# A hybrid recurrent, retention and convolution block on one core: activation operands made in parts, values in single banks, a weight unit queued behind the last norm

## The chip, the cores and the metric

The kernel runs on one core of one Trainium2 chip. The metric is the device time of one execution in microseconds (us); lower is better. A core has TensorE (PE: matmuls, with weight loads shown apart as PEld), VectorE (DVE), ScalarE (ACT), GpSimd (POOL) and SyncE (SP, which issues the DMAs here). Each works through its own queue in order. Matmuls write to PSUM, which has eight banks of 512 float32 columns on each of 128 partitions; everything else lies in SBUF.

## The reference

One layer over 528 tokens (16 meta tokens and 512 of the sequence), width 1024. All inputs are float32.

```python
xn = rms_norm(h, norm_mix_g[l])
z = xn @ w_in[l]
u_rnn, u_gate, q, k, v, g_ret, ga, gb = jnp.split(z, IN_SPLITS, axis=-1)
xr = causal_dwconv(u_rnn, rnn_conv_w[l], rnn_conv_b[l])
hr = rg_lru(xr, ...)
o_a = hr * jax.nn.gelu(u_gate)
q = rotary(q, pos); k = rotary(k, pos) * (RET_DK ** -0.5)
o = retention(q, k, v)
o_b = head_rms(o) * jax.nn.silu(g_ret)
mixed = sigmoid(ga) * (o_a @ w_branch_rnn[l]) + sigmoid(gb) * (o_b @ w_branch_ret[l])
h = h + mixed @ w_out[l]
xn = rms_norm(h, norm_ffn_g[l])
up = causal_dwconv(xn @ w_up[l], ffn_conv_w[l], ffn_conv_b[l])
gate, val = jnp.split(up, 2, axis=-1)
h = h + (jax.nn.gelu(gate) * val) @ w_down[l]
out = rms_norm(h, norm_final_g)[:, N_META:]
```

There are four retention heads with 512 values each; the feed-forward width is 3072, so `w_up` has 6144 columns (gates, then values).

## The kernel before

Every matmul runs on float16. An operand is split into a high and a low half, `hi` on ACT (line 92) and the rest `lo` on DVE (line 93), in the helper `split`; a product is the sum of three float16 products. Weights come in units of up to 1 MB, loaded by SP into two raw buffers (`wraw`), each load issued behind the one before it, and split into tiles `wt` of a pool of ten (`wsp`). `get(u)` makes all splits up to unit u at that point of the program, `tick()` makes one more step if not too many tiles are ahead.

Some products are Strassen forms: seven products of sums of blocks in place of eight. Their weight units are marked `fast`, have four tiles and need three sums on DVE (lines 255 to 257).

The program is traced in Python order. Up to line 713 the order on PE, ACT and DVE is the traced one; from there on a scheduler fixes each engine's order ahead of time, by the program's order (its priority), by what it takes to be ready, and by explicit edges. `tc.high_priority()` moves instructions ahead, `tc.issue_after(x)` queues those of the block that are on x's engine behind x, without a wait for x's result. A tile pool of PSUM, SBUF or raw buffers makes the next user of a slot wait for the last one.

The places that the change and the prediction touch, in order of time:

- `values(h)`, from line 884 on, the values of one head: five blocks of up to 128 tokens by 512 columns. Blocks 0 to 3 take 24 matmuls each (line 907), block 4, the last 16 tokens, 16 small ones (line 899) that read every weight tile of the head. Two blocks share a two-bank tile of the pool `acc`: block 0 and 1, 2 and 3. Each block is then split to `v` (lines 92 and 93). From head 2 on, PSUM is laid out as two such tiles and four single banks of the pool `bank`; the gates' products (`pa`, `pe`, `pb` of `fast_products`, line 844) take the single banks. Heads run as `gated(0)`, `values(2)`, `gated(1)`, `values(3)`, `gated(2)`.
- `out_proj(i)`, lines 1172 to 1189, for four blocks of 128 tokens: product (line 1180), residual `h` (line 1185), and the second norm's rows by `norm_rows`: Square and Sqrt on ACT (lines 343, 345), reciprocal and the two halves of `xo` on DVE (lines 347, 353). PE transposes `xo` later in `out_norm` (line 360). The loop after it calls `tick()` once for each block.
- Then `early`: three half products (line 408) with the first up unit `u_up[0][0]` (two) and the second, `u_up[0][1]` (one). The last norm's transposes are queued behind the second half product.
- The up projection, a loop over j = 0 to 11. Units j = 3, 5, 7, 9 (`FAST_UP`) form the gates by `up_products`: seven products (line 1319) into `pa`, `pe`, `pb`. `pa` is built up further after each copy of its state by ACT (`keep`, line 1325, into `kept`, `last`, `g`), and DVE adds (`add`, line 1329). The values use plain products (line 395). Convolutions are at lines 1295 and 1297, gelu at line 1311, gate times value at 1384 or 1395.
- At the end of each j, `act_forms` makes the operands of the down projection: four differences `d`, `y` of 256 columns on DVE (lines 1261 to 1264), and splits of A11 (256 columns) and of A12/A22, `y` and `d` (512 columns each) into `a` and `act`. They are used only by the down projection, after j = 11.

Of the kernel before, what the change touches and what calls it, by code (L numbers as in the profile page):

```python
# [9 lines left out]
F16 = mybir.dt.float16  # L10
AF = mybir.ActivationFunctionType
# [3 lines left out]
P = 128  # L15
# [36 lines left out]
def hybrid_block_kernel(ctx, tc, x, meta, norm_mix_g, w_in, conv_w, conv_b, rg_a_w, rg_a_b,  # L52
# [21 lines left out]
    def acc(name):  # L74
        return psum["acc"].tile([P, 2, 512], F32, name=name, tag="acc")
# [219 lines left out]
    def tick(n=1):  # L295

        for _ in range(n):
            if done[0] == len(steps):
                if len(loaded) == len(units):
                    return  # L300
                queue(unit_load())
            u = steps[done[0]][0]
            if sum(unit_tiles(i) for i in range(current[0], u + 1)) > ahead[0]:
                return
            emit_step()
# [34 lines left out]
    def rms_scale(src, rows, name):  # L340
        junk = work.tile([P, D], F16, name="junk", tag="w")
        ss = small.tile([P, 1], F32, name="ss")
        nc.scalar.activation(junk[:rows], src, AF.Square, accum_out=ss[:rows])
        sd = small.tile([P, 1], F32, name="sd")
        nc.scalar.activation(sd[:rows], ss[:rows], AF.Sqrt, scale=1.0 / D, bias=eps_t[:rows])
        rs = small.tile([P, 1], F32, name="rs")
        nc.vector.reciprocal(rs[:rows], sd[:rows])
        return rs

    def norm_rows(src, rows, g_bc, xn):  # L350
        rs = rms_scale(src, rows, "n")
        for a in range(2):
            nc.vector.scalar_tensor_tensor(xn[a][:rows], src[:, a * 512:(a + 1) * 512], rs[:rows], g_bc[a][:rows],
                                           op0=ALU.mult, op1=ALU.mult)

    def norm_transpose(rows, xhd, xld, s, xn):
        for a in range(2):
# [526 lines left out]
    def values(h):  # L884
        vt = []
        wa, wb = get(u_v[h][0]), get(u_v[h][1])
        for b, (j0, nb) in enumerate(JB):
            if b % 2 == 0:
                ps = acc("ps")
            pb = ps[:, b % 2]  # L890
            vt.append(piece([P, 2, 512], F16, f"v{h}"))
            i = 0
            if b == 4:
                for r, wr in enumerate((wa, wb)):
                    for a in range(2):
                        for g in range(4):
                            m = 2 * NM if a == 0 else NM
                            xs = xlast[:, 4 * r + g].rearrange("p a t -> p (a t)")
                            nc.tensor.matmul(pb[32 * g:32 * g + m], xs[:, :m], wr(a, g, 0, 512),
                                             start=r == 0 and a == 0, stop=r == 1 and a == 1,  # L900
                                             tile_position=(0, 32 * g))
                split(vt[b][:, 0], vt[b][:, 1], pb, S_V / (SW * S_XN))
                continue
            for k in range(KD):
                w = wa if k < 4 else wb
                for ax, aw in SPLIT:
                    nc.tensor.matmul(pb, xf(ax, k, XF + j0, nb), w(aw, k % 4, 0, 512), start=i == 0, stop=i == 23)  # L907
                    i += 1
            split(vt[b][:, 0], vt[b][:, 1], pb, S_V / (SW * S_XN))
            tick()  # L910
        vv[h] = vt
# [257 lines left out]

    psum_layout(bank=2, acc=3)  # L1170

    def out_proj(i):
        ps = acc("ps")
        halo = acc("ps") if i == 1 else None
        c0 = 2 + P * i
        ks = (0, 1, 2, 3, 4, 5, 7, 6) if i == 0 else range(KD)
        for k in ks:
            for n in range(2):
                for a, aw in SPLIT:
                    nc.tensor.matmul(ps[:, n], mx[k][:, a, c0:c0 + P], wo[k // 2](aw, k % 2, n * 512, 512),  # L1180
                                     start=k == 0 and (a, aw) == (0, 0), stop=k == ks[-1] and a == 1)
                if halo is not None:
                    halo_part(halo, k, 4 * n)
        hv = h2[i].rearrange("p (a b) -> p a b", a=2)
        nc.vector.scalar_tensor_tensor(hv, ps, 1.0 / (SW * S_MX), hv, op0=ALU.mult, op1=ALU.add)
        xn = pair("xo")
        with tc.high_priority():
            norm_rows(h2[i], P, gffn, xn)
        return xn, halo

    def out_norm(i, xn):
# [36 lines left out]
    for i in range(1, 4):  # L1228
        xn, halo = out_proj(i)
        xns.append(xn)  # L1230
        if i == 1:
            halo_sum(halo)
        out_norm(i - 1, xns[i - 1])
        tick()
        if i == 2:
            halo_finish()
    x2_whole(0)
# [6 lines left out]

    early = {}
    for ch, (u, col) in enumerate(((u_up[0][0], 0), (u_up[0][0], P), (u_up[0][1], 0))):
        wv = get(u)
        early[ch if ch < 2 else KF] = ps = acc("ps")
        mm = project_half(ps, wv, col, x2f, HU, 0)
        if ch == 1:  # L1250
            with tc.high_priority(), tc.issue_after(mm):
                out_norm(3, xns[3])
# [3 lines left out]
    def act_forms(j, vals):  # L1256


        (h1, h2_), (t0, t1) = halves, vals
        d, y = gates_t("d"), gates_t("y")  # L1260
        nc.vector.tensor_tensor(d[:, h2_], t0[:, h2_], t1[:, h2_], op=ALU.subtract)
        nc.vector.tensor_tensor(y[:, h1], t0[:, h1], t0[:, h2_], op=ALU.subtract)
        nc.vector.tensor_tensor(d[:, h1], t0[:, h1], d[:, h2_], op=ALU.subtract)
        nc.vector.tensor_tensor(y[:, h2_], d[:, h1], t1[:, h1], op=ALU.subtract)
        if j % 2 == 0:
            a11_t.append(piece([P, 2, SEQ], F16, "a11"))
        a11 = a11_t[-1][:, :, 256 * (j % 2):256 * (j % 2) + 256]
        split(a11[:, 0], a11[:, 1], t0[:, h1], S_ACT)
        at = {"A11": (a11, 0)}
        if j >= 10:  # L1270
            if j == 10:
                a21_t.append(piece([P, 2, SEQ], F16, "a21"))
            a21 = a21_t[0][:, :, 256 * (j % 2):256 * (j % 2) + 256]
            split(a21[:, 0], a21[:, 1], t0[:, h2_], S_ACT)
            at["A21"] = (a21, 0)
        for src, s, nms in ((t1, S_ACT, ("A12", "A22")), (y, S_ACT, ("F7", "F3")), (d, -S_ACT, ("F6", "F5"))):
            t = piece([P, 2, SEQ], F16, "act")
            split(t[:, 0], t[:, 1], src[:, :SEQ], s)
            at.update({nm: (t, 256 * i) for i, nm in enumerate(nms)})
        acts.append(at)  # L1280

    def gates_t(name):
        return work.tile([P, T], F32, name=name, tag="w")
# [30 lines left out]
    def up_products(w):  # L1314

        def product(ps, wf, xf_, first=False):
            for k in range(4):
                for aw, ax in SPLIT:
                    nc.tensor.matmul(ps[:, :258], w(wf, aw, k), x2_form(xf_, ax, k),  # L1319
                                     start=first and k == 0 and (aw, ax) == (0, 0), stop=k == 3 and aw == 1,  # L1320
                                     skip_group_check=True)

        def keep(dst, ps):
            with tc.high_priority():
                nc.scalar.activation(dst, ps[:, :258], AF.Copy)

        def add(dst, ps, k):
            with tc.high_priority():
                nc.vector.tensor_tensor(dst, ps[:, :258], k, op=ALU.add)

        kept, g0, g1 = (piece([P, 2, 258], F32, nm) for nm in ("kept", "g0", "g1"))
        last = piece([P, 258], F32, "last")
        pa = acc("pa")[:, 0]
        product(pa, "B11", "A11", True)
        keep(kept[:, 0], pa)
        yield
        pe = bank("pe")
        product(pe, "T3", "F7", True)
        yield
        product(pa, "T2", "F6")  # L1340
        keep(kept[:, 1], pa)
        yield
        pb = bank("pb")
        product(pb, "B21", "A12", True)
        add(g0[:, 0], pb, kept[:, 0])
        yield
        product(pa, "T1", "F5")
        keep(last, pa)
        add(g1[:, 1], pe, last)
        yield  # L1350
        product(pa, "B22", "F3")
        keep(g1[:, 0], pa)
        yield g1
        product(pe, "T4", "A22")
        add(g0[:, 1], pe, kept[:, 1])
        yield g0

    forming = []

    def forms(n):  # L1360
        for _ in range(n if forming else 0):
# [2 lines left out]
    for j in range(12):  # L1364
# [6 lines left out]
        gates, vals = [], []  # L1371
        if j in FAST_UP:
            run = up_products(wg)
            for _ in range(5):
                next(run)
                tick()
            vals.append(up_conv(wu, 0, KF + 2 * j))
            tick()
# [6 lines left out]
        else:  # L1385
# [4 lines left out]
            for m in range(2):  # L1390
# [5 lines left out]
                vals.append(cv)  # L1396
                tick()
                forms(1)
        act_forms(j, vals)


    ahead[0] = 9
# [178 lines left out]
```

## Time and profile before

| | |
|---|---|
| median of 3 runs | 1072.78 us (1072.77 to 1072.82) |
| profiled execution | 1072.88 us, span 1071.2 us |
| PE busy | 1051.1 us (98%) |
| PEld busy | 851.3 us (79%) |
| DVE busy | 863.1 us (81%) |
| ACT busy | 584.1 us (55%) |
| granted TensorE clock, mean | 0.999 |

The span runs from the first to the last instruction of the program; the rest of the profiled execution's time lies around it. Busy times are of each engine's own instructions; an idle engine that nobody waits for costs nothing.

### The profile page before, as it was taken

The page shows a single profiled execution, that of the slowest core. Times are in us where ns is not written, and L with a number is a line of the kernel's source. Part 1 is how long each engine was busy: PE and PEld are TensorE (multiplying, and loading weights), DVE is VectorE, ACT ScalarE, POOL GpSimd, SP SyncE. Part 2 cuts the span into 40 slices and gives each one's busy share as a digit, 9 for nine tenths or more (in the row PEclk, how much of TensorE's full clock was granted, in tenths as well). Part 3 has the DMA queues.
Part 4 walks back from the last instruction along what each step waited for, and adds up shares of the span by engine and source line. Part 5 has one row for each costly group of instructions (what it writes and reads, how often), then busy time and mean ns, then how long its engine had stood idle before and what let it go on. Part 6 is the DMA issues. An engine that isn't in the chain of part 4 may idle for free.

```text
span 1071.2 us, 20996 instructions
## 1 busy us (share of the span) xinstructions
PE 1051.1 (98%) x8995; PEld 851.3 (79%) x8995; DVE 863.1 (81%) x1297; ACT 584.1 (55%) x903; POOL 6.9 (1%) x20
## 2 busy tenths in 40 slices
PE   9999999999999999999999999999999999999997
PEld 6888888865684858888888885588888888888884
DVE  6884799998786969877797785599888887988875
ACT  8558954434564747566454453364555465454442
POOL 2000000000000000000000000000000000000000
PEclk9999999999999999999999999999999999999999
DMA  8341243431212222423333355032331423214322
GB/s 254 105 133 41 80 138 119 159 120 40 80 41 69 90 64 65 128 90 119 103 104 119 119 199 176 33 124 74 126 119 62 137 80 119 80 59 131 107 80 79
DMA packets 108990, 111.49 MB, mean 104 GB/s; under 512 B 5611, under 2 KB 100561, under 8 KB 108897
## 3 DMA queue, kind: packets, MB, share of 16 engines
q1 hardware_dynamic: 108448, 109.74, 31.8%
q8 instruction: 70, 1.15, 0.5%
q10 hardware_dynamic: 160, 0.27, 0.1%
q0 software_dynamic: 288, 0.14, 0.1%
q14 instruction: 24, 0.19, 0.1%
HBM read 108.04 MB, written 2.10 MB: 103 GB/s over the span
## 4 chain that ended last, share of the span: by engine, by line
PE 73%; DVE 16%; ACT 9%; issue 2%; ACTq 0%; DVEq 0%
PE ps L395 28%; PE P L1417 9%; PE pa L844 9%; PE pm L395 4%; PE ps L907 4%; PE ps L1180 4%; DVE wt L93 4%; PE pe L844 4%; PE ps L408 2%; PE pb L844 2%; ACT wt L92 2%; PE pa L1319 2%; PE ps L929 1%; DVE rnn L642 1%; DVE raw L255 1%
## 5 line engine op out<-in xcount | busy, mean ns | idle before, releaser
L395 PEld LDWEIGHTS <-wt 128*128 128x128 f16 x3840 | 373.2, 97 | 58.2 <-DVE t L736 1.4
L93 DVE SCALAR_TENSOR_TENSOR wt<-raw,wt 128x1024 f16<-128x1024 f32 (+2 forms) x278 | 303.8, 1105 | 69.1 <-ACT wt L92 68.0
L92 ACT ACTIVATE wt<-raw 128x1024 f16<-128x1024 f32 (+2 forms) x278 | 262.9, 961 | 152.6 <-PE P L1417 25.3
L844 PEld LDWEIGHTS <-wt 128*128 128x128 f16 x2016 | 195.1, 97 | 34.7 <-issue 7.4
L395 PE MATMUL ps<-x2h,wt 128*128 128x258 f16 x1184 | 182.0, 273 | 0.0
L395 PE MATMUL ps<-xh,wt 128*128 128x257 f16 (+2 forms) x1056 | 163.8, 275 | 1.1 <-DVE t L736 1.1
L395 PE MATMUL ps<-x2l,wt 128*128 128x258 f16 x592 | 113.3, 272 | 0.0
L395 PE MATMUL ps<-xl,wt 128*128 128x257 f16 (+2 forms) x528 | 102.2, 275 | 0.0
L1417 PE MATMUL P<-wt,act 128*128 128x256 f16 x792 | 88.3, 273 | 0.0
L1417 PEld LDWEIGHTS <-act 128*128 128x128 f16 x792 | 77.5, 98 | 9.0
L907 PE MATMUL ps<-wt,xh 128*128 128x512 f16 x256 | 76.1, 379 | 2.3 <-DVE v L93 2.3
L844 PE MATMUL pa<-xs,wt 128*128 128x257 f16 x576 | 71.6, 273 | 3.4 <-ACT kept L849 3.1
L1297 DVE SCALAR_TENSOR_TENSOR cv<-ps,vt,cv 128x512 f32<-128x512 f32 x80 | 59.7, 746 | 16.5 <-ACT cv L1295 15.8
L395 PE MATMUL pm<-oa,wt 128*128 128x257 f16 x480 | 55.4, 274 | 0.0
L907 PEld LDWEIGHTS <-xh 128*128 128x128 f16 x256 | 24.8, 98 | 31.4 <-issue 3.4
L907 PE MATMUL ps<-wt,xl 128*128 128x512 f16 x128 | 48.3, 379 | 0.0
L255 DVE TENSOR_TENSOR raw<-raw 128x1024 f32<-128x1024 f32 x39 | 47.6, 1220 | 0.7
L844 PE MATMUL pa<-ob,wt 128*128 128x257 f16 x384 | 45.7, 274 | 0.6 <-ACT last L849 0.5
L1180 PE MATMUL ps<-wt,mx 128*128 128x512 f16 x192 | 44.3, 379 | 0.0
L1295 ACT ACTIVATE cv<-ps,vt,vt 128x512 f32<-128x512 f32 x40 | 30.8, 769 | 23.4 <-PE ps L395 18.5
L1319 PEld LDWEIGHTS <-wt 128*128 128x128 f16 x336 | 32.6, 97 | 8.5 <-issue 4.1
L1180 PEld LDWEIGHTS <-mx 128*128 128x128 f16 x192 | 17.6, 98 | 18.5
(288 smaller groups left out, 1414.6 us busy)
## 6 DMA issues: line engine op xcount, KB each, us to landing
raw<-in_w_in SPq DMA_DIRECT2D x40, 1024.0 KB, 4.9
raw<-in_w_up SPq DMA_DIRECT2D x24, 1024.0 KB, 5.3
raw<-in_w_down SPq DMA_DIRECT2D x48, 256.0 KB, 3.5
raw<-in_w_branch_ret SPq DMA_DIRECT2D x16, 512.0 KB, 4.6
raw<-in_w_branch_rnn SPq DMA_DIRECT2D x8, 640.0 KB, 4.7
raw<-in_w_out SPq DMA_DIRECT2D x4, 1024.0 KB, 5.1
xin<-in_x SPq DMA_DIRECT2D x4, 512.0 KB, 5.8
raw<-in_w_in SPq DMA_DIRECT2D x4, 512.0 KB, 8.3
```

The lines of the kernel that those rows point to most:

```text
L92: nc.scalar.activation(hi, src, AF.Copy, scale=s)
L93: nc.vector.scalar_tensor_tensor(lo, src, s, hi, op0=ALU.mult, op1=ALU.subtract)
L255: nc.vector.tensor_tensor(pair, pair, rv[:, :, right].rearrange("p (h k) c -> p h k c", h=2), op=ALU.add)
L395: nc.tensor.matmul(ps[:, hf, :n], w(aw, k, col, P), src(ax, k, c0, n), start=k == 0 and (aw, ax) == (0, 0), stop=k == nk - 1 and aw == 1)
L408: mm = nc.tensor.matmul(ps[:, hf, :n], w(aw, k, col, P), src(ax, k, c0, n), start=k == 0 and (aw, ax) == (0, 0), stop=k == KD - 1 and aw == 1)
L844: nc.tensor.matmul(ps[:, :257], ws[k // 4](wf, aw, k % 4), src(xf_, ax, k), start=first and k == 0 and (aw, ax) == (0, 0), stop=k == last_ ...
L907: nc.tensor.matmul(pb, xf(ax, k, XF + j0, nb), w(aw, k % 4, 0, 512), start=i == 0, stop=i == 23)
L1180: nc.tensor.matmul(ps[:, n], mx[k][:, a, c0:c0 + P], wo[k // 2](aw, k % 2, n * 512, 512), start=k == 0 and (a, aw) == (0, 0), stop=k == ks ...
L1295: nc.scalar.activation(vv_, src[:, :, 2:258], AF.Identity, scale=vt2[:, 96 + ch:97 + ch], bias=bias)
L1297: nc.vector.scalar_tensor_tensor(vv_, src[:, :, j:j + 256], vt2[:, 48 * j + ch:48 * j + ch + 1], vv_, op0=ALU.mult, op1=ALU.add)
L1319: nc.tensor.matmul(ps[:, :258], w(wf, aw, k), x2_form(xf_, ax, k), start=first and k == 0 and (aw, ax) == (0, 0), stop=k == 3 and aw == 1, ...
L1417: nc.tensor.matmul(pd[:, 256 * tt:256 * tt + 256], t[:, ax, c0 + tt * P:c0 + tt * P + P], w(wf, aw, i), start=q % 6 == 0 and tt == 0 and i ...
```

## The change

In `act_forms` the work is put into three functions: `differences` (the four differences), `plain` (A11, A21 where there is one, and A12/A22) and `formed` (`y` and `d`). They go on a list. If the next j is not in `FAST_UP` they run at once, in the order in which they stood; if it is, `flush` runs the first behind the fourth of the next j's products and the other two behind the fifth, queued behind the latest copy on ACT and the latest sum on DVE. For heads 2 and 3 `values` takes one single bank for each block in place of half a two-bank tile. `norm_rows` returns its Sqrt and its last DVE instruction; the loop's `tick()` is left out for the last block, and the splits of `u_up[0][1]` are queued behind those two instructions.

```diff
-        nc.scalar.activation(sd[:rows], ss[:rows], AF.Sqrt, scale=1.0 / D, bias=eps_t[:rows])
+        root[0] = nc.scalar.activation(sd[:rows], ss[:rows], AF.Sqrt, scale=1.0 / D, bias=eps_t[:rows]).ins
...
+        return root[0], rr.ins
...
-            if b % 2 == 0:
-                ps = acc("ps")
-            pb = ps[:, b % 2]
+            if h >= 2:
+                pb = bank("pv")
+            else:
+                if b % 2 == 0:
+                    ps = acc("ps")
+                pb = ps[:, b % 2]
...
-            norm_rows(h2[i], P, gffn, xn)
+            behind[0] = norm_rows(h2[i], P, gffn, xn)
...
-        tick()
+        if i < 3:
+            tick()
...
-        wv = get(u)
+        if ch < 2:
+            wv = get(u)
+        else:
+            with tc.issue_after(behind[0][0]), tc.issue_after(behind[0][1]):
+                wv = get(u)
...
+        return [differences, plain, formed]
...
-                nc.scalar.activation(dst, ps[:, :258], AF.Copy)
+                last_copy[0] = nc.scalar.activation(dst, ps[:, :258], AF.Copy).ins
...
-                nc.vector.tensor_tensor(dst, ps[:, :258], k, op=ALU.add)
+                last_sum[0] = nc.vector.tensor_tensor(dst, ps[:, :258], k, op=ALU.add).ins
...
+    def flush(n):
+
+        for _ in range(min(n, len(pending))):
+            with tc.issue_after(last_copy[0]), tc.issue_after(last_sum[0]):
+                pending.pop(0)()
...
-            for _ in range(5):
+            for n in range(5):
                 next(run)
+                if n in (3, 4):
+                    flush(n - 2)
                 tick()
...
-        act_forms(j, vals)
+        pending.extend(act_forms(j, vals))
+        if j + 1 not in FAST_UP:
+            while pending:
+                pending.pop(0)()
```

## Rows read from the trace of the kernel before

**Rows 1.** The page of the profile, its first part: busy time, share of the span and number of instructions of each engine.

```profile
PE 1051.1 (98%) x8995; PEld 851.3 (79%) x8995; DVE 863.1 (81%) x1297; ACT 584.1 (55%) x903; POOL 6.9 (1%) x20
```

**Rows 2.** The view of waits, of TensorE (PE) over the whole span: who waited for whom, total in us, times, longest in us.

```profile
PE pa L844 <- ACT kept L849: 3.1, 5, 1.1
PE pa L1319 <- ACT kept L1325: 2.6, 4, 0.7
PE ps L907 <- DVE v L93: 2.3, 3, 1.4
PE ptr L360 <- DVE xo L353: 0.6, 1, 0.6
```

**Rows 3.** The timeline from 762 to 775 us, in and around the products of the first Strassen unit of the up projection (j = 3): start us, length us, engine, line, operation, what it writes and reads, number of instructions merged, and in brackets the engine's idle time before it and who ended it.

```profile
763.66 0.27 PE L1319 MATMUL pa<-x2h,wt 128*128 128x258 f16 x1
...
766.83 0.63 ACT L92 ACTIVATE act<-cv 128x512 f16<-128x512 f32 x1 [1.87 <-DVE cv L1395]
...
769.31 0.38 PE L395 MATMUL ps<-x2l,wt 128*128 128x258 f16 x2
769.37 0.63 ACT L92 ACTIVATE act<-y 128x512 f16<-128x512 f32 x1 [1.92 <-DVE y L1264]
...
769.91 0.61 ACT L92 ACTIVATE act<-d 128x512 f16<-128x512 f32 x1
...
770.43 0.37 ACT L1325 ACTIVATE kept<-pa 128x258 f32<-128x258 f32 x1
770.85 1.49 PE L1319 MATMUL pa<-x2f,wt 128*128 128x258 f16 x12 [0.70 <-ACT kept L1325]
```

**Rows 4.** The view of waits, of the weight loads (PEld) from 700 to 960 us, columns as in rows 2.

```profile
PEld L1319 <- issue: 4.1, 8, 0.9
```

**Rows 5.** The groups of instructions from 700 us to the end, of the splits of the activations' operands and of their differences: line, engine, operation, tiles, shapes, count, busy us, mean ns of one, idle time before them.

```profile
L93 DVE SCALAR_TENSOR_TENSOR act<-y,act 128x512 f16<-128x512 f32 x12 | 8.2, 687 | 0.8 <-ACT act L92 0.7
L92 ACT ACTIVATE act<-y 128x512 f16<-128x512 f32 x12 | 7.6, 630 | 18.5 <-DVE y L1264 18.5
L93 DVE SCALAR_TENSOR_TENSOR a<-cv,a 128x256 f16<-128x256 f32 x14 | 5.7, 416 | 0.5 <-ACT a L92 0.5
L92 ACT ACTIVATE a<-cv 128x256 f16<-128x256 f32 x14 | 5.5, 410 | 4.6 <-DVE cv L1395 3.7 <-DVE cv L1384 0.9
L1261 DVE TENSOR_TENSOR d<-cv 128x256 f32<-128x256 f32 x12 | 5.0, 417 | 0.0
```

**Rows 6.** Busy time of each engine by stretch: stretch in us, its length, then for PE, PEld, DVE, ACT and POOL the busy us with the number of instructions, the granted clock, the DMA share and GB/s. First two stretches of the values and gates of heads 1 to 3, then three of the up projection.

```profile
346.00:371.00 25.00, 24.95 (x250) 21.90 (x249) 23.21 (x33) 17.70 (x31) 0.00 (x0) 1.00 0.38 125
393.00:430.50 37.50, 36.29 (x339) 30.67 (x338) 37.19 (x55) 27.55 (x47) 0.00 (x0) 1.00 0.27 82
705.00:762.00 57.00, 57.00 (x515) 49.81 (x513) 55.40 (x83) 32.16 (x46) 0.00 (x0) 1.00 0.29 95
763.00:775.00 12.00, 11.27 (x101) 9.60 (x99) 8.71 (x15) 5.06 (x10) 0.00 (x0) 1.00 0.30 95
778.00:805.00 27.00, 27.00 (x245) 23.55 (x243) 23.87 (x35) 15.38 (x22) 0.00 (x0) 1.00 0.37 117
```

**Rows 7.** The timeline of the values of head 2 (one row) and of head 3, and the wait that comes after the latter; columns as in rows 3.

```profile
331.18 0.59 PE L907 MATMUL ps<-wt,xh 128*128 128x512 f16 x2 [0.49 <-DVE v L93]
...
381.44 0.68 DVE L93 SCALAR_TENSOR_TENSOR v<-ps,v 128x512 f16<-128x512 f32 x1
382.17 0.59 PE L907 MATMUL ps<-wt,xh 128*128 128x512 f16 x2 [1.45 <-DVE v L93]
...
391.71 1.06 ACT L92 ACTIVATE wt<-raw 128x1024 f16<-128x1024 f32 x1 [2.27 <-PE ps L907]
392.79 3.12 DVE L93 SCALAR_TENSOR_TENSOR wt<-raw,wt 128x1024 f16<-128x1024 f32 x3 [2.63 <-ACT wt L92]
...
395.17 0.38 PE L907 MATMUL ps<-wt,xl 128*128 128x512 f16 x1
...
430.52 1.49 PE L844 MATMUL pa<-xs,wt 128*128 128x257 f16 x12 [1.06 <-ACT kept L849]
```

**Rows 8.** The timeline from 692 to 704 us, around the last norm and the first product with the second up unit; columns as in rows 3.

```profile
692.45 25.95 SPq L103 DMA_DIRECT2D raw<-in_w_up  x4
...
697.51 1.06 ACT L343 ACTIVATE junk<-h 128x1024 f16<-128x1024 f32 x1
698.55 1.05 ACT L92 ACTIVATE wt<-raw 128x1024 f16<-128x1024 f32 x1
...
699.49 0.29 ACT L345 ACTIVATE sd<-ss,eps_t 128x1 f32<-128x1 f32 x1
699.63 1.23 DVE L93 SCALAR_TENSOR_TENSOR wt<-raw,wt 128x1024 f16<-128x1024 f32 x1 [1.11 <-ACT wt L92]
...
700.85 1.21 DVE L93 SCALAR_TENSOR_TENSOR wt<-raw,wt 128x1024 f16<-128x1024 f32 x1
701.97 1.41 DVE L353 SCALAR_TENSOR_TENSOR xo<-h,rs,gffn 128x512 f32<-128x512 f32 x2
702.86 0.63 PE L360 MATMUL ptr<-ident,xo 128*128 128x128 f32 x4 [0.65 <-DVE xo L353]
...
703.33 0.27 PE L408 MATMUL ps<-x2h,wt 128*128 128x258 f16 x1
```

**Rows 9.** The page, part 6: DMA issues of the up projection's weights, KB each, median us from issue to landing.

```profile
raw<-in_w_up SPq DMA_DIRECT2D x24, 1024.0 KB, 5.3
```

More of the change, by code (lines that the diff above doesn't have):

```diff
@@ L348, in rms_scale @@
         return rs
+    root = [None]
     def norm_rows(src, rows, g_bc, xn):
@@ L352, in norm_rows @@
         for a in range(2):
-            nc.vector.scalar_tensor_tensor(xn[a][:rows], src[:, a * 512:(a + 1) * 512], rs[:rows], g_bc[a][:rows],
-                                           op0=ALU.mult, op1=ALU.mult)
+            rr = nc.vector.scalar_tensor_tensor(xn[a][:rows], src[:, a * 512:(a + 1) * 512], rs[:rows], g_bc[a][:rows],
+                                                op0=ALU.mult, op1=ALU.mult)
+        return root[0], rr.ins
     def norm_transpose(rows, xhd, xld, s, xn):
@@ L1170, in hybrid_block_kernel @@
     psum_layout(bank=2, acc=3)
+    behind = [None]
     def out_proj(i):
@@ L1259, in act_forms, with differences, both @@
         (h1, h2_), (t0, t1) = halves, vals
[L1260 to L1276, printed above, removed]
+        at, tmp = {}, {}
+        acts.append(at)
+        def differences():
+            d, y = tmp["d"], tmp["y"] = gates_t("d"), gates_t("y")
+            nc.vector.tensor_tensor(d[:, h2_], t0[:, h2_], t1[:, h2_], op=ALU.subtract)
+            nc.vector.tensor_tensor(y[:, h1], t0[:, h1], t0[:, h2_], op=ALU.subtract)
+            nc.vector.tensor_tensor(d[:, h1], t0[:, h1], d[:, h2_], op=ALU.subtract)
+            nc.vector.tensor_tensor(y[:, h2_], d[:, h1], t1[:, h1], op=ALU.subtract)
+        def both(src, s, nms):
             t = piece([P, 2, SEQ], F16, "act")
@@ L1279, in act_forms, with plain, formed @@
             at.update({nm: (t, 256 * i) for i, nm in enumerate(nms)})
-        acts.append(at)
+        def plain():
+            if j % 2 == 0:
+                a11_t.append(piece([P, 2, SEQ], F16, "a11"))
+            a11 = a11_t[-1][:, :, 256 * (j % 2):256 * (j % 2) + 256]
+            split(a11[:, 0], a11[:, 1], t0[:, h1], S_ACT)
+            at["A11"] = (a11, 0)
+            if j >= 10:
+                if j == 10:
+                    a21_t.append(piece([P, 2, SEQ], F16, "a21"))
+                a21 = a21_t[0][:, :, 256 * (j % 2):256 * (j % 2) + 256]
+                split(a21[:, 0], a21[:, 1], t0[:, h2_], S_ACT)
+                at["A21"] = (a21, 0)
+            both(t1, S_ACT, ("A12", "A22"))
+        def formed():
+            both(tmp["y"], S_ACT, ("F7", "F3"))
+            both(tmp["d"], -S_ACT, ("F6", "F5"))
+        return [differences, plain, formed]
     def gates_t(name):
@@ L1356, in up_products @@
         yield g0
-    forming = []
+    forming, pending = [], []
+    last_copy, last_sum = [None], [None]
+    def flush(n):
+        for _ in range(min(n, len(pending))):
+            with tc.issue_after(last_copy[0]), tc.issue_after(last_sum[0]):
+                pending.pop(0)()
     def forms(n):
```

## The prediction

> **What bounds the kernel now.** I read the page's busy times first: TensorE (PE) is busy 1051.1 of 1071.2 us, VectorE (DVE) 863.1, ScalarE (ACT) 584.1 [rows 1]. PE is the path, no matmul is added or taken away, so the change can only give back time in which PE stands still: about 20 us, start and tail included. The view of waits then says for whom PE stands: 2.6 us for `kept` at line 1325, 2.3 us at the values for the splits of `v`, 0.6 us for the last norm's rows `xo`; a further 3.1 us, at line 844, belongs to gates that the change leaves alone [rows 2]. Third, the timeline around each wait, and the stretches' busy times, to see what stands in the queue ahead of the instruction that ends it.
>
> **How long a stall is.** A lone row of a 258-column matmul lasts 0.27 us, two merged last 0.38 [rows 3, 8]: each costs 0.11 us of PE, and the last 0.16 of its row lies beside the next one. So the idle figure ahead of a stalled matmul is 0.16 us short. At 770.85 us the idle is 0.70, the stall 0.86. The idle times of the weight loads, which have no such tail, confirm it: 4.1 us at line 1319, in eight waits [rows 4], where the matmul rows say 2.6 in four. Besides the four long waits of about 0.8 us (3.2 in all) they hold four short ones of 0.2. The Trainium skill, "Perfetto Trace Analysis", section "Tensor Engine Instruction (MATMUL, LD_WEIGHTS)", says that a matmul's end is computed by the profiler, not observed; the trace agrees, since rows overlap. By the idle column alone the three parts would hold 2.6 + 2.3 + 0.6 = 5.5 us at most; by starts they hold 7.2, as follows.
>
> **Part 1, operands behind the copies** (units j = 3, 5, 7, 9). The first product's matmuls end at about 763.9, but its copy `kept` runs at 770.43: ahead of it in ACT's queue stand the operand splits of unit j = 2, of which one waits 1.87 us for DVE's product and one 1.92 us for the difference `y` [rows 3]. PE fills the time with the up value's matmuls and then stalls. The change queues the differences behind the fourth product's sum and the splits behind the copy of the fifth. Nothing is added; what moves, per unit, is on ACT 3 x 0.63 + 0.41 = 2.3 us, on DVE 3 x 0.69 + 0.42 + 4 x 0.42 = 4.2 us [rows 5]. No DMA moves, and SP and POOL have no part in it. New waits: ACT's `act <- y` and `act <- d` still wait for DVE's differences, and behind them in the queue now stand the sixth product's copy and the convolutions; nobody on PE waits for that copy soon, since the next products go to other banks. The moved work has cover: from 763 to 775 us DVE is busy 8.71 of 12 us, ACT 5.06; from 778 to 805 DVE 23.87 of 27 [rows 6]. If the first slack goes unused, 4.2 us meet the 3.1 us left in the second, and 1.1 us per unit would be late. Bounds: all of the 4.1 us [rows 4], or 3.2 less about half of it for copies that now find one weight split (about 1.05 us, as in rows 8) ahead of them: 1.6. I take 3.5: the long waits gone, the short ones mostly kept.
>
> **Part 2, values of heads 2 and 3 in single banks.** A pair of blocks shares a two-bank tile, and the second block's matmuls wait until DVE has split the first: DVE's split runs from 381.44, PE goes on at 382.17 after 1.45 us; for head 2 it is 0.49 [rows 7]. With the 0.16 each: 1.61 + 0.65 = 2.26 us. With one bank per block, and four banks in the pool, neither wait has a cause, as the gates' three banks come free within the first block. Does the gain last? After head 2, DVE is busy 23.21 of 25 us, so it has 1.8 us of room and can follow a PE that is 0.65 early. After head 3, DVE is busy 37.19 of 37.50 us, and that stretch ends in a PE wait of 1.06 us, for a `kept` behind splits that hang on DVE [rows 6, 7]. There DVE sets the time, and an earlier PE only waits longer, unless DVE's run starts earlier. It starts at 392.79 with splits of the next weights, which wait for PE to leave the values' weight tiles (ACT at 391.71) [rows 7]. Before, block 4, short but reading all weights, ran ahead of block 3; without the wait the order is likely 0 to 4, so the tiles come free only at the very end: 395.4 less 2.3, about 393.1, up to 1.4 us later than 391.71. Bounds: +2.26, or 0.65 - 1.4 = -0.75. I take the middle, +0.7. The Trainium skill, "Perfetto Trace Analysis", section "Matmuls", has independent groups rotate through PSUM banks so that the evacuation of one overlaps the next; by that alone the part would give its 2.26, and it is the first rival below.
>
> **Part 3, the second up unit behind the last norm.** The chain is Square at 697.51, root at 699.49, rows `xo` at 701.97, transposes at 702.86 after 0.65 us of idle: a stall of 0.81 [rows 8]. A weight split of 1.05 us on ACT stands ahead of the root, two of 1.22 on DVE ahead of `xo`. Are they the second unit's? SP issues its next load of up weights at 692.45, and a load lands 5.3 us later, at 697.75 [rows 8, 9]: the split at 698.55 looks like that load's, so a later unit's, and the new edges don't hold it. What they do hold, the second unit's two splits (2 x 1.05 on ACT, 2 x 1.22 on DVE), now comes behind the root and behind `xo`. If `xo` still ends at 703.38, the third product, which starts at 703.33 [rows 8], waits up to 1.2 us for its first lower half; if `xo` comes 1.5 us earlier it waits for nothing. Also the raw buffer stays taken some 10 us longer, so one of the four loads that SP issues from 692.45 to 718 goes later; their units are used a whole j later (four column blocks of 48 matmuls at 0.11 us, 21 us of PE), which hides it. DVE, busy 55.40 of 57 us from 705 to 762 [rows 6], takes the rest of the 2.4 us out of weight splits made well ahead. Bounds +0.81 and -1.2; both ends being equally near, the middle: -0.2.
>
> **Sum.** 3.5 + 0.7 - 0.2 = 4.0 us. The profiled execution took 1072.88 us (span 1071.2 and 1.7 around it); the median is 1072.78, 0.1 less. 1072.8 - 4.0 = 1068.8 us. About 0.2%, or 2.1 us, is what a measurement of this kernel tells from no change.
>
> **Rivals.**
> - All stalls gone for good: 4.1 + 2.3 + 0.8 = 7.2, so 1065.6 us. For it: each stall has one visible cause. Against: DVE's full stretch after head 3. Chance 0.15.
> - Exchange: the copies or sums now wait behind other work (weight splits on ACT, the moved differences on DVE), and part 1 gives 1.0 in place of 3.5, part 2 and 3 together 0.5: 1071.3 us. For it: PE has stood behind such splits in the gates too [rows 2]. Against: 3.3 us of idle DVE from 763 to 775. Chance 0.2.
> - DVE becomes the bound of the up projection (slower): its moved 4.2 us per unit find less room than thought. It decides from the point where over 0.9 us a unit, what part 1 wins, is late. If half of the 3.1 us of room can't be used, 2.6 us a unit are late, 1.8 net, in four units 7: 1079 us. Against: nothing on PE waits for the operands until the down projection. Chance 0.06.
> - Part 3 does not do what it says, as its own step argues: within the forecast, 0.2 to 0.8 us either way.
>
> **How the numbers follow.** Forecast 0.55, the rest of 0.04 spread. Faster by over 0.2%: 0.55 + 0.15 and 0.01 of the spread, 0.71; within: the exchange and 0.01, 0.21; slower: 0.06 and 0.02, 0.08. The range goes from 1065.6, every stall gone, to 1071.8, past the exchange by part 2's lower end.
>
> **What would show it.** Right: no wait of line 1319 for `kept` over 0.3 us, ACT's `act` splits behind `last`; no wait of line 907 for `v` in heads 2 and 3, but a longer one near 430 us; at the last norm, whether a split still stands between Square and root, and whether the third half product waits for its weights. Wrong: new waits of PE for weights or accumulators between 700 and 950 us, or a changed order in the gates that moves the 3.1 us there.

## The result, and the profile after

The changed kernel takes 1076.51 us (median of 7 runs, 1074.57 to 1078.0) against 1072.8 of the kernel before in the same session (7 runs, 1072.7 to 1073.65): ratio 1.003, 95% interval 1.0018 to 1.0041. It is slower by 3.7 us, where 4.0 us of gain were forecast, and lies outside the range. The profiled execution took 1077.32 us, its span is 1075.6. Of the runs in the experiments below, one of e3 (1096.84 us) and one of the kernel before (2213.81 us) were slow and are left out of every ratio.

TensorE's busy time is as before [rows 1]: no work was added, the 4.4 us are PE standing still or running at its lower clock. The page of after, busy times and chain of work:

```profile
PE 1051.3 (98%) x8995; PEld 851.8 (79%) x8995; DVE 864.0 (80%) x1297; ACT 583.1 (54%) x903; POOL 6.9 (1%) x20
...
PE 65%; DVE 19%; ACT 10%; DMA 4%; issue 2%; ACTq 0%; SPq 0%; DVEq 0%
```

The same line of the chain in the kernel before, which named no DMA:

```profile
PE 73%; DVE 16%; ACT 9%; issue 2%; ACTq 0%; DVEq 0%
```

Who PE waits for in after, over the whole span (total us, times, longest); it answers to [rows 2]:

```profile
PE pa L847 <- ACT kept L852: 7.9, 10, 1.5
PE pa L847 <- ACT last L852: 2.5, 3, 1.6
PE pa L1345 <- ACT kept L1351: 2.1, 1, 2.1
...
PE ps L411 <- DVE wt L93: 0.5, 1, 0.5
...
PE ps L913 <- DVE v L93: 0.3, 1, 0.3
```

Most of the waits at which the change aimed are gone: that for `xo` (0.6), both for `v` in heads 2 and 3 (the 0.3 us that is left of 2.3 belongs to an earlier head, which the change leaves alone) and, at the up projection, three of the four long ones for `kept`. In their place stand 10.4 us in the gates (line 847, before line 844 with 3.1 + 0.5) and one wait of 2.1 us at j = 3 (line 1345, before line 1319).

Where the time went is seen best by setting the start of the n-th matmul of after against the n-th of before (both have 8995):

| place (us in before) | after is late by |
|---|---|
| 400, behind the values of head 3 | -1.7 us (it is ahead) |
| 444, within the gates | 0.0 |
| 461 | 1.8 |
| 478 | 3.4 |
| 648, behind the last gates | 4.3 |
| 708, early half products | 4.5 |
| 775, products of j = 3 | 7.4 |
| behind j = 5, 7, 9 | 6.4, 5.4, 4.4 |
| end | 4.4 |

So part 2 first gained some 1.5 us (0.2 of the 1.7 stood at 300 us already) and then lost that and 4.3 us more in the gates. Of these, 0.6 came at 645 us, behind a load of `w_out` that took 6.3 us to land where it took 4.8 before; e2 and e14, which also have part 2, lose nothing there. At j = 3, where part 1 should have gained, 2.9 us were lost, and 0.2 at the norm, both to part 3; part 1 gave 1.0 in each of the other three units.

**The gates.** The load of before that the reading turns on, from its timeline:

```profile
444.06 0.37 SPq L103 DMA_DIRECT2D raw<-in_w_in  x1
```

After's timeline: the start of the next head's weight splits (which wait for PE to leave the values' tiles, as in [rows 7]), SP's next load, and the costliest wait:

```profile
392.80 1.05 PE L905 MATMUL pv<-wt,xlast 128*32 128x512 f16 x16
393.45 1.06 ACT L92 ACTIVATE wt<-raw 128x1024 f16<-128x1024 f32 x1
...
450.10 0.37 SPq L103 DMA_DIRECT2D raw<-in_w_in  x1
...
455.99 0.63 ACT L92 ACTIVATE wt<-raw 128x512 f16<-128x512 f32 x1 [7.17 <-DMA raw<-in_w_in]
456.52 0.37 ACT L852 ACTIVATE last<-pa 128x257 f32<-128x257 f32 x1
...
456.94 1.49 PE L847 MATMUL pa<-xs,wt 128*128 128x257 f16 x12 [1.63 <-ACT last L852]
```

Block 4 (line 905) now runs last of the five, and the split that waits for it starts at 393.45, not at 391.71 [rows 7]. The load that before left at 444.06 leaves at 450.10. Its split then stands at the head of ACT's queue and waits 7.17 us for the data, and behind it waits `last`, for which PE stands 1.63 us.

**The up projection at j = 3.** After's timeline: SP's loads, and ACT ahead of the copy `kept`; it answers to [rows 3] and [rows 8]:

```profile
710.92 0.38 SPq L103 DMA_DIRECT2D raw<-in_w_up  x1
...
716.88 0.37 SPq L103 DMA_DIRECT2D raw<-in_w_up  x1
...
725.91 0.37 SPq L103 DMA_DIRECT2D raw<-in_w_up  x1
...
758.83 0.37 SPq L103 DMA_DIRECT2D raw<-in_w_up  x1
763.62 0.37 SPq L103 DMA_DIRECT2D raw<-in_w_up  x1
...
764.08 1.06 ACT L92 ACTIVATE wt<-raw 128x1024 f16<-128x1024 f32 x1 [2.79 <-DMA raw<-in_w_up]
...
768.16 0.27 PE L1345 MATMUL pa<-x2h,wt 128*128 128x258 f16 x1
...
768.85 1.06 ACT L92 ACTIVATE wt<-raw 128x1024 f16<-128x1024 f32 x1 [1.58 <-DMA raw<-in_w_up]
...
770.47 1.04 ACT L92 ACTIVATE wt<-raw 128x1024 f16<-128x1024 f32 x1
...
771.42 0.37 ACT L1351 ACTIVATE kept<-pa 128x258 f32<-128x258 f32 x1
771.85 0.82 PE L1345 MATMUL pa<-x2f,wt 128*128 128x258 f16 x6 [2.08 <-ACT kept L1351]
```

The first load behind the norm leaves at 710.92 instead of 692.45 [rows 8], 14 us late if the program's own 4.4 us are taken off. What it waited for is seen in the splits. In before the second unit's splits run ahead of the last norm: on ACT the first of them at 687.17, on DVE the second's lower half as the first of two in a merged row, ending at 692.42:

```profile
687.17 1.05 ACT L92 ACTIVATE wt<-raw 128x1024 f16<-128x1024 f32 x1
...
691.20 2.35 DVE L93 SCALAR_TENSOR_TENSOR wt<-raw,wt 128x1024 f16<-128x1024 f32 x2
```

In after they come behind the root, and in ACT's row the third unit's two splits, which the program makes after the second's, come with them:

```profile
703.21 3.88 ACT L92 ACTIVATE wt<-raw 128x1024 f16<-128x1024 f32 x4
...
709.63 1.22 DVE L93 SCALAR_TENSOR_TENSOR wt<-raw,wt 128x1024 f16<-128x1024 f32 x1
```

So both raw buffers stay taken. The second unit's last lower half ends at 710.85 and the load leaves at 710.92; the third's ends at 716.80 and the next load leaves at 716.88. In before, after, e2, e3, e6 and e12 every load of up weights from 690 to 800 us leaves 0.03 to 0.07 us behind the end of a lower half on DVE. The activations' splits are gone from ahead of `kept`, as planned, but from 764 us on weight splits stand there, two of which wait for data that has not landed. The Trainium skill, "TensorE: Matmul & The Clock Gate", section "Architectural detail: the array is 16× 32×32, not 1× 128×128", says that ACT takes its instructions strictly in order; the trace agrees: the last matmul that `kept` needs starts at 768.16, yet `kept` runs at 771.42, behind a split that waits 1.58 us for its load, a convolution and another split.

**The clock.** Windows of after behind that wait (stretch, length, busy us of PE, PEld, DVE, ACT, POOL, granted clock, DMA share, GB/s):

```profile
768.00:771.90 3.90, 1.82 (x17) 1.46 (x16) 3.80 (x6) 2.95 (x4) 0.00 (x0) 1.00 0.79 248
771.90:773.40 1.50, 1.50 (x14) 1.28 (x14) 1.50 (x2) 0.09 (x1) 0.00 (x0) 0.94 0.23 72
773.40:776.70 3.30, 3.30 (x17) 2.33 (x16) 3.27 (x6) 0.81 (x2) 0.00 (x0) 0.51 0.56 162
776.70:780.00 3.30, 3.30 (x32) 2.88 (x30) 2.67 (x6) 2.32 (x5) 0.00 (x0) 1.00 0.47 158
```

Behind 2.08 us of idling the granted clock falls to 0.51, its 1.2 GHz level, for one stretch of 3.3 us, in which 17 matmuls run; the next 3.3 us hold 32. The 15 that are missing are 15 x 0.11 = 1.65 us. The other 1.4 us at j = 3 are the wait: 2.25 where 0.86 stood. After's seven runs lie in two groups: three from 1074.57 to 1074.93 with a mean clock of 0.998 to 0.999, and four from 1076.51 to 1078.0 with 0.995 to 0.997; the profiled one is of the second. It seems that the clock falls in some executions and not in others, though only one of them has a trace.

### The profile page after: what moved, and what is told of

It is laid out like the page before. It is cut to its first block, busy times and chain, and to the rows that moved or that the text cites. A ratio compares the mean times of both kernels' runs of the same rounds, so it can differ in the third digit from the quotient of the medians.

```text
span 1075.6 us, 20978 instructions
## 1 busy us (share of the span) xinstructions
PE 1051.3 (98%) x8995; PEld 851.8 (79%) x8995; DVE 864.0 (80%) x1297; ACT 583.1 (54%) x903; POOL 6.9 (1%) x20
## 4 chain that ended last, share of the span: by engine, by line
PE 65%; DVE 19%; ACT 10%; DMA 4%; issue 2%; ACTq 0%; SPq 0%; DVEq 0%
PE ps L398 24%; PE P L1455 9%; PE pa L847 6%; DVE wt L93 5%; PE ps L1188 4%; PE pv L913 4%; PE pm L398 3%; ACT wt L92 3%; PE pe L847 2%; PE ps L913 2%; DMA raw<-in_w_up 2%; PE pa L1345 2%; DMA raw<-in_w_in 1%; PE ps L411 1%; PE pb L847 1%
## 5 line engine op out<-in xcount | busy, mean ns | idle before, releaser
L398 PEld LDWEIGHTS <-wt 128*128 128x128 f16 x3840 | 373.1, 97 | 58.3 <-DVE t L739 1.4
L847 PEld LDWEIGHTS <-wt 128*128 128x128 f16 x2016 | 195.0, 97 | 42.0 <-issue 15.2
L1345 PEld LDWEIGHTS <-wt 128*128 128x128 f16 x336 | 33.5, 100 | 7.5 <-issue 2.3
L913 PE MATMUL ps<-wt,xh 128*128 128x512 f16 x128 | 38.0, 379 | 0.3 <-DVE v L93 0.3
L913 PE MATMUL pv<-wt,xh 128*128 128x512 f16 x128 | 38.1, 379 | 0.0
L411 PEld LDWEIGHTS <-wt 128*128 128x128 f16 x288 | 27.8, 97 | 6.3 <-DVE wt L93 1.0
```

The source lines that it names most:

```text
L398: nc.tensor.matmul(ps[:, hf, :n], w(aw, k, col, P), src(ax, k, c0, n), start=k == 0 and (aw, ax) == (0, 0), stop=k == nk - 1 and aw == 1)
L411: mm = nc.tensor.matmul(ps[:, hf, :n], w(aw, k, col, P), src(ax, k, c0, n), start=k == 0 and (aw, ax) == (0, 0), stop=k == KD - 1 and aw == 1)
L847: nc.tensor.matmul(ps[:, :257], ws[k // 4](wf, aw, k % 4), src(xf_, ax, k), start=first and k == 0 and (aw, ax) == (0, 0), stop=k == last_ ...
```

## Experiments

Each ratio is against runs of the kernel before on the same chip. The median of before was 1073.08 us for the first four kernels, 1072.85 for the next four, 1072.76 for the last three. The diffs are against the changed kernel where nothing else is said.

| kernel | median us | against before | ratio, 95% interval |
|---|---|---|---|
| e1, part 1 alone | 1068.92 | -4.2 | 0.996 (0.9947 to 0.9973) |
| e2, part 2 alone | 1076.43 | +3.4 | 1.0031 (1.0019 to 1.0043) |
| e3, part 3 alone | 1079.09 | +6.0 | 1.0052 (1.0038 to 1.0067) |
| e4, part 2 with block 4 ahead of block 3 | 1072.11 | -1.0 | 0.9989 (0.998 to 0.9999) |
| e5, part 1 and e4's values | 1068.09 | -4.8 | 0.9959 (0.9947 to 0.9972) |
| e6, fourth unit held in place of the second | 1071.95 | -0.9 | 0.9991 (0.9983 to 1.0) |
| e10, parts 1 and 3 | 1071.23 | -1.6 | 0.999 (0.9981 to 0.9999) |
| e11, part 1, e4's values, e6's hold | 1067.18 | -5.7 | 0.9947 (0.9935 to 0.996) |
| e12, part 3's edges alone | 1078.19 | +5.4 | 1.005 (1.0033 to 1.0067) |
| e13, part 3's tick alone | 1072.79 | 0.0 | 1.0 (0.999 to 1.0009) |
| e14, parts 1 and 2 | 1072.42 | -0.3 | 0.9997 (0.9987 to 1.0006) |

The theory after the result: parts 2 and 3 remove their waits, but delay the freeing of weight tiles or raw buffers; loads then leave late, and their splits block ACT ahead of copies that PE waits for. The rivals: the parts only lose together, or DVE is the bound.

**e1: part 1 alone.** The two other parts undone:

```diff
-            if h >= 2:
-                pb = bank("pv")
-            else:
-                if b % 2 == 0:
-                    ps = acc("ps")
-                pb = ps[:, b % 2]
+            if b % 2 == 0:
+                ps = acc("ps")
+            pb = ps[:, b % 2]
...
-        if i < 3:
-            tick()
+        tick()
...
-            with tc.issue_after(behind[0][0]), tc.issue_after(behind[0][1]):
-                wv = get(u)
+        wv = get(u)
```

> Part 1 alone: the operands in parts behind the copies, values and norm as before. Theory (each part acts by itself; the wait of 2.1 us in unit j = 3 of the changed kernel belongs to part 3): all eight waits of line 1319 go, 4.1 us, 1068.7 us (1068.3 to 1069.5), granted clock 1.00 throughout. Rival (the moved splits themselves make ACT or DVE late in the first fast unit): a wait of 1 to 2 us for kept in j = 3 stays, with or without a drop of the clock: 1070.5 to 1074 us.

4.2 us faster by the medians, 4.0 by the spans (1067.2 against 1071.2). The views of waits from 690 to 960 us, PE and weight loads, hold only the norm now; all eight waits of [rows 4] are gone, the short ones too:

```profile
PE ptr L363 <- DVE xo L355: 0.6, 1, 0.6
```

e1's ACT at j = 3: one weight split stands ahead of the first `kept`, and the activations' splits run behind `last`:

```profile
763.47 1.05 ACT L92 ACTIVATE wt<-raw 128x1024 f16<-128x1024 f32 x1
764.42 0.38 ACT L1343 ACTIVATE kept<-pa 128x258 f32<-128x258 f32 x1
...
769.35 0.39 ACT L1343 ACTIVATE last<-pa 128x258 f32<-128x258 f32 x1 [2.26 <-PE pa L1337]
769.63 1.05 ACT L92 ACTIVATE wt<-raw 128x1024 f16<-128x1024 f32 x1
770.58 0.41 ACT L92 ACTIVATE a<-cv 128x256 f16<-128x256 f32 x1
```

**e2: part 2 alone.** The change to `values` only: e1's last two hunks, and the operands made at once:

```diff
-                if n in (3, 4):
-                    flush(n - 2)
...
-        if j + 1 not in FAST_UP:
-            while pending:
-                pending.pop(0)()
+        while pending:
+            pending.pop(0)()
```

> Part 2 alone: values of heads 2 and 3 in single banks. Theory (the heads' weight tiles, and so the next splits and loads, come free only behind block 4, and the gates pay for it): the waits of the values go (2.3 us), the gates up to 480 us lose about 6: 1077 us (1076 to 1078). Rival (DVE's full stretch only takes the gain back, the rest of the loss in the changed kernel is a chance of its order): 1072 to 1073 us.

3.4 us slower. PE's waits between 300 and 600 us in e2 (before: 3.1 for `kept`, 1.9 for `v`):

```profile
PE pa L847 <- ACT kept L852: 7.1, 8, 1.5
PE pa L847 <- ACT last L852: 1.5, 2, 1.2
```

The two waits for `v` are gone and over 5 us of new ones in the gates have come, with SP's loads as late as in after (450.20 for 444.06). Part 2 loses without the other two.

**e4: the same, with block 4 ahead of block 3.** It tells whether the order of the blocks, and with it the time at which the weight tiles come free, is the loss. The diff is against e2:

```diff
-        for b, (j0, nb) in enumerate(JB):
+        for b in ((0, 1, 2, 4, 3) if h >= 2 else range(5)):
+            j0, nb = JB[b]
```

> Part 2 alone, but with block 4 of heads 2 and 3 traced ahead of block 3, so that block 3 leaves the weight tiles one after another. Theory (release of the weight tiles is what part 2 loses by): the waits of the values stay away, the gates wait about as before, 1070.5 to 1072 us. Rival (single banks cost the gates in another way, through the banks that pa, pe and pb need): 1075 us or more, as for part 2 by itself.

1.0 us faster than before (0.1 above the expected range), 4.3 us faster than e2. In e4 the splits start while block 3 still runs, 4.2 us earlier than e2's 393.48, and the waits of the gates shrink (PE's waits from 300 to 600 us):

```profile
389.31 1.06 ACT L92 ACTIVATE wt<-raw 128x1024 f16<-128x1024 f32 x1 [0.79 <-PE pv L914]
```

```profile
PE pa L847 <- ACT kept L852: 4.7, 7, 1.4
```

The load of the gates that left at 450.20 in e2 leaves at 442.93. The loss of part 2 is the late freeing of the tiles. Of the 2.26 us that the two waits held, 0.8 to 1.0 last; the rest goes to waits for `kept`, of 1.43 and 0.64 us behind the values of head 3, where before had 1.06 alone. In the first, `kept` stands on ACT behind a weight split that waits 0.79 us for its load; in the second, behind a split of `y` that waits 1.59 us for DVE.

**e3: part 3 alone.** e1's hunk in `values` and e2's two hunks, so that this is left of the change:

```diff
         out_norm(i - 1, xns[i - 1])
-        tick()
+        if i < 3:
+            tick()
...
+            with tc.issue_after(behind[0][0]), tc.issue_after(behind[0][1]):
+                wv = get(u)
```

> Part 3 alone: second up unit's splits behind the last norm. Theory (the later units' splits and loads stand behind it, since tiles and raw buffers go round in order, and meet the copies of unit j = 3): the wait for xo goes, about 1 us is lost at the third half product, and unit j = 3 waits 2 us or more, with a drop of the clock behind it: 1075 to 1077 us. Rival (part 3 is neutral, its loads catch up by 760 us): 1072 to 1073 us.

6.0 us slower, 2.1 us past the slow end of the expected range. The wait for `xo` is gone, the third half product waits 0.53 us for its weights, and at j = 3 PE stands for 4.23 us. e3's windows there, with the clock's fall behind it:

```profile
770.00:774.80 4.80, 0.65 (x6) 0.42 (x5) 4.80 (x10) 2.02 (x4) 0.00 (x0) 1.00 0.69 218
774.80:778.00 3.20, 3.12 (x17) 2.29 (x17) 1.24 (x3) 0.41 (x2) 0.00 (x0) 0.59 0.00 0
778.00:781.00 3.00, 3.00 (x26) 2.46 (x25) 0.43 (x1) 1.17 (x2) 0.00 (x0) 0.87 0.00 0
```

Here both kinds of splits stand ahead of the copy: late weight splits, then the activations', which part 1 would have moved.

**e12 and e13: the two edits of part 3 apart.** e12 keeps the edges and the last tick, e13 drops the tick and has no edges. Against e3, e12 and then e13:

```diff
-        if i < 3:
-            tick()
+        tick()
```

```diff
-            with tc.issue_after(behind[0][0]), tc.issue_after(behind[0][1]):
-                wv = get(u)
+        wv = get(u)
```

> Kernel before with half of part 3: the edges that hold the second up unit behind the root and the last norm's rows, with the tick after the fourth chunk kept. Theory (part 3 loses by the edges: the held unit keeps two raw buffers, so the loads come some 14 us late and meet the copies at j = 3): as part 3 alone, about 1079 us, the first up load behind the norm after 705 us, a wait of 2 to 5 us for kept near 773 us. Rival (the loss comes from the dropped tick, which puts every later weight step one place back): about 1072.3 to 1073, loads as before.

> Kernel before with the other half of part 3: the tick after the fourth chunk dropped, no edges. Theory (edges lose): within 0.7 us of before, up loads from about 692 us on, no wait over 1 us at j = 3. Rival (the dropped tick loses): 1075 to 1079 us with a wait of 2 us or more for kept near 773 us.

The edges lose, 5.4 us, the tick alone does nothing. e12's edges even hold only half of the unit: with the tick kept, the first of the second unit's two splits still runs ahead of the norm, at 687.30 on ACT, and the second comes at 699.02. In e12 the first up load behind the norm leaves at 704.35 (a little before the 705 expected), and PE waits 3.64 us for `kept` at j = 3. One more wait, which nobody expected, comes at 715.03: 1.25 us for DVE's convolution.

**e6: another unit held.** It tells whether holding a unit back is the loss, or holding this one. Against the kernel before, with `behind` set as in the change, in the function that makes a weight unit's next step:

```diff
-        run()
+        if u == u_up[1][1]:
+            with tc.issue_after(behind[0][0]), tc.issue_after(behind[0][1]):
+                run()
+        else:
+            run()
```

> Kernel before with one thing added: not the second but the fourth up unit's two splits are held behind the last norm's root and rows; the second unit is made as before and every other order stays. Theory (the split that stood between Square and root belongs to a later unit, and the loss of part 3 comes from holding the second unit, which holds the raw buffers and the loads behind it): PE's wait of 0.65 us for xo shrinks to under 0.3, the third half product doesn't wait, the up loads move by less than 4 us and no wait over 1 us appears at j = 3: 0.5 to 0.8 us faster, about 1072.4. Rival (any unit held behind the norm makes the loads late enough to meet the copies at j = 3): 1075 to 1079 us, with a wait of 2 us or more for kept near 772 us.

0.9 us faster, a little more than expected. e6's timeline at the norm (before: [rows 8]):

```profile
692.12 0.38 SPq L103 DMA_DIRECT2D raw<-in_w_up  x1
...
694.51 0.37 SPq L103 DMA_DIRECT2D raw<-in_w_up  x1
...
698.12 0.20 ACT L347 ACTIVATION_READ_ACCUMULATOR junk<-h 128x1 f32 x1
698.36 0.29 ACT L349 ACTIVATE sd<-ss,eps_t 128x1 f32<-128x1 f32 x1
698.56 3.88 ACT L92 ACTIVATE wt<-raw 128x1024 f16<-128x1024 f32 x4
...
698.88 1.41 DVE L359 SCALAR_TENSOR_TENSOR xo<-h,rs,gffn 128x512 f32<-128x512 f32 x2
...
701.72 1.04 PE L367 MATMUL ptr<-ident,xo 128*128 128x128 f32 x8
```

The root follows Square, `xo` ends 3.1 us earlier, and the transposes have no idle time ahead of them. The two loads at 692 and 694 us keep their time. The next is 7.2 us later than before (709.28 for 702.08), more than the 4 us expected, and by 733 us the loads are back at their old times (732.98 for 734.23). So a delay of one load is recovered; a delay of the whole chain from 692 us on is not.

**e10: parts 1 and 3.** It tells whether j = 3 needs part 2's delays as well. The values are as before:

```diff
-            if h >= 2:
-                pb = bank("pv")
...
+            if b % 2 == 0:
+                ps = acc("ps")
+            pb = ps[:, b % 2]
```

> Parts 1 and 3 without part 2. Theory (part 3's loss arises at j = 3 from late loads, whatever the values do; part 1 removes the splits ahead of the copies there, so only the late weight splits are left): 4.0 gained by part 1 at j = 5, 7, 9 and partly at j = 3, a wait of about 2 us for kept and a fall of the granted clock behind it at j = 3: about 1072 us (1071 to 1073.5). Rival (the late loads need part 2's delays as well to collide): 1069 us, no wait over 1 us at j = 3. Rival (the losses add: -4.0 + 6.0): 1075 us.

1.6 us faster, so part 3 costs 2.5 us on top of part 1. The wait at j = 3 is there, 2.37 us, behind a weight split that waits 1.53 us for its load and another. But in the profiled execution (1071.40 us) the clock does not fall behind it; e10's windows:

```profile
765.20:767.60 2.40, 0.05 (x1) 0.00 (x0) 2.40 (x3) 2.37 (x4) 0.00 (x0) 1.00 1.02 335
767.60:771.00 3.40, 3.38 (x31) 2.98 (x31) 3.33 (x6) 0.91 (x2) 0.00 (x0) 1.00 0.26 76
```

That part of the expectation fell for this execution. The eleven runs again lie in two groups: eight from 1070.78 to 1071.63 (clock 0.998 to 0.999), three from 1073.12 to 1073.57 (0.997), where the clock seems to have fallen; none of the three has a trace.

**e14: parts 1 and 2 as changed.** After without part 3:

```diff
-        if i < 3:
-            tick()
+        tick()
...
-            with tc.issue_after(behind[0][0]), tc.issue_after(behind[0][1]):
-                wv = get(u)
+        wv = get(u)
```

> The changed kernel without part 3: parts 1 and 2 as changed. Theory (the parts add): 1072.9 - 4.0 + 3.4, about 1072.3 us, no wait over 0.3 us in the units j = 3, 5, 7 and 9, granted clock 1.00 there. Rival (part 2's delays alone make the loads late enough at j = 3): 1074 us or more.

1072.42, as the theory had it: parts 1 and 2 add, and no wait is left at j = 3 to 9. With part 3 the kernel takes 4.1 us more, by medians of different sessions, against 2.5 in e10. The groups account for the difference: the runs of after with the higher clock lie 2.2 to 2.5 us above e14, those of e10 1.9 to 2.7 above e1, and after's median run is one with the lower clock, e10's is not.

**e5 and e11: better versions.** e5 is part 1 with e4's values, e11 has e6's hold as well; e5 is e14 with e4's diff, e11 is e5 with e6's.

> Part 1 as changed, values of heads 2 and 3 in single banks with block 4 traced ahead of block 3, last norm and second up unit as before. Theory (the parts are independent; part 2's loss is the late freeing of the weight tiles by block order alone): part 1 alone gave 4.0 us, the other block order 0.8: 1073.1 - 4.8, about 1068.2 us, no wait of TensorE over 0.3 us in units j = 3, 5, 7 and 9. Rival (DVE is the bound behind head 3, so a gain of the values is lost again by the up projection): as part 1 alone, 1069.0 or a little above. Rival (the parts disturb each other, as the three together did): above 1070.

> Part 1, values in single banks with block 4 ahead of block 3, and the fourth up unit's splits (not the second's) held behind the last norm. Theory: the gains add, 4.0 + 0.8 + 0.6 = 5.4 us, about 1067.6 us. Rival (holding the fourth unit delays the loads too): 1069 to 1072 us with a new wait at j = 3.

1068.09 and 1067.18: the gains add, both within 0.5 us of the theory. e11 is 5.7 us faster than the kernel before and 9.3 faster than the changed one. PE's waits over its span have no line of the norm or the up projection left; of the parts that the change touches these remain:

```profile
PE pa L851 <- ACT kept L856: 4.6, 7, 1.4
...
PE pa L851 <- ACT last L856: 0.8, 2, 0.5
PE ps L918 <- DVE v L93: 0.4, 1, 0.4
```

## Why the prediction was wrong

**How long a stall is.** Right: the 4.1 us that the weight loads' view showed for part 1's eight waits came back as 4.0 to 4.2. Adding 0.16 us to the idle column gives 3.2 of it, the four long waits; the rest is the four short ones. One slip: the 2.3 us for `v` in the sum by the idle column hold 0.3 of an earlier head that the change leaves alone; the forecast itself uses only the two waits of heads 2 and 3.

**Part 1** (forecast 3.5, measured 4.0 to 4.2). The step was right, the size near its upper bound: the short waits, which I had mostly kept, went too, since a single weight split ahead of `kept` at 763.47 does not hold it up. The rival that DVE becomes the bound fell: its moved work found room, and e1 has no wait in these units.

**Part 2** (forecast +0.7, measured -3.4 alone). The step failed at the lower bound, 0.65 - 1.4. Its facts held: block 4 ran last, the tiles came free 1.7 us later (1.4 were forecast), and of the 2.26 us some 1.5 had arrived at 400 us in after and were lost again by 444, as the step feared. Even where the tiles come early (e4) only 0.8 to 1.0 lasts, though DVE ends only one of e4's two new waits there, and a late load the other. What I left out is that the delay doesn't stop at that split. The split frees a raw buffer, the next load waits for it, and its own split is later again: the loads of the gates leave 2.2, 3.9, 3.1, 6.1, 1.2 and 6.0 us late (397.53, 415.09, 418.70, 433.44, 435.24, 450.10 for 395.34, 411.16, 415.56, 427.39, 434.00, 444.06), each 0.03 to 0.07 us behind the end of a lower half on DVE, in after as in before. I counted what a late split costs DVE, and not the loads behind it nor the copies behind those loads' splits. Why 2 us grow to 6 there was not followed step by step. Late loads alone are not enough: behind head 2's values two loads of after leave 2.5 and 5.0 us late as well (347.04 and 353.17 for 344.56 and 348.19), the next but one is early again (371.77 for 373.64), and PE loses nothing up to 400 us.

**Part 3** (forecast -0.2, measured -6.0 alone, -2.5 beside part 1, -4.1 beside parts 1 and 2). Right was that the split between Square and root is a later unit's: e6 holds only the fourth unit and clears the norm. It was cleared in after too, as all later splits came behind the held ones. Right in size was the third half product's wait (0.53 of idle). The step that failed is the sentence that one of the four loads goes later and that its unit's use a whole j later hides it. Not one load but all from 692 us on moved, the first by 14 us: the third unit's splits follow the held ones in order, so not one raw buffer but both stayed taken, and for these two units DVE's last lower halves ended 5.6 and 9.7 us behind ACT's halves (2.9 and 2.8 in before). And a unit's use on PE is not the first place where a late load hurts: its split stands in ACT's queue at its old place, and the copies that PE waits for stand behind it, long before PE wants the weights. e12 shows that the edges do it, e13 that the dropped tick does not.

**The sum and the rivals.** That the parts could lose was bounded by -0.75 and -1.2; both bounds were taken from the durations of the moved instructions, none from a load that comes late, and no rival had that mechanism. The exchange rival (0.2) came nearest: it has the copies wait behind weight splits on ACT, but as a smaller gain, 1.0 us for part 1, and not because the splits wait for their loads. The slower rival (0.06) named DVE in the up projection, which did not happen. Of what would make the prediction wrong, "new waits of PE" from 700 us on and "a changed order in the gates" were named, without a price. The clock's 1.65 us were not thought of.

What stays open is why the clock fell behind 2.08 us of idling in after's profiled execution and not behind 2.37 us in e10's; no kernel has a trace from both of its groups. That part 3's lateness is the raw buffers' is read from the times at which loads leave, 0.03 to 0.07 us behind the lower halves; a third raw buffer, which would test it, was not tried.

## What to carry to other kernels

Before an instruction that frees a buffer is held back, follow the chain behind it: the load that waits for the buffer, the loads that wait in turn behind that one, and the place of each load's first consumer in its engine's queue; price the delay there, not at the matmul that needs the data last. Where one of several independent blocks reads all the weights, order the blocks so that the weights come free early; here that alone was worth 4.3 us. Of work that must give way, try the unit whose use is furthest off: here, the one case tried, the fourth unit held in place of the second turned 6.0 us of loss into 0.9 of gain.

## What the runs showed of the hardware that was not expected

The granted clock fell to its lower level behind single idle times of TensorE in an otherwise full stretch: behind 2.08 us in after and behind 4.23 and 3.64 us in e3 and e12, at a cost of 1.65 us in after. In the profiled executions it did not fall behind the gates' waits of 1.5 to 1.6 us in after, nor behind 2.37 us in e10. e3's four compared runs and e12's four lie within 0.7 us of each other, while after and e10, with the middle waits, have two groups of runs some 2 us apart. The Trainium skill, "TensorE: Matmul & The Clock Gate", section "What's actually happening", says that the chip's watch over TensorE runs on its own and isn't started with the kernel, so that the moment of a change differs from run to run; the two groups fit that, but no run here shows the watch itself.
